# Ten plain single slices in front, a VectorE fill and a new hand-written order in a Strassen weight-gradient matmul

## The chip, the cores and the metric

The kernel runs on one core of one Trainium2 chip. The metric is device time in microseconds (us), the median of several executions. The core's engines are TensorE (PE, with its weight loads shown apart as PEld), VectorE (DVE), ScalarE (ACT), GpSimd (POOL) and SyncE (SP). Each has an instruction queue of its own that runs in order; semaphores tie the queues together.

## The reference

```python
batch, m, k, n = 16, 512, 1024, 768
input:       (16, 512, 1024) float32, randn
grad_output: (16, 512, 768)  float32, randn

def reference(input, grad_output):
    return np.einsum('bmk,bmn->kn', input, grad_output).astype(np.float32)
```

One product of a 1024 x 8192 matrix (the transposed input X) with an 8192 x 768 matrix (grad_output G). The contraction runs over 8192 rows, so every row is read once and everything is summed into one 1024 x 768 result.

## The kernel before

**Slices, pairs, loads.** The 8192 rows are 64 slices of 128 rows. A load is a pair of slices, 32 loads in all. The string `LOADS` (line 12) says what is done with each: `s` is plain, `P` goes through one level of Strassen's scheme in Winograd's form. Before, loads 0 to 3 and the last one are plain, the 27 between are Strassen pairs. All loads but the first slice are DMAs from the GpSimd queue that round float32 to bf16 on the way. Loads below `MERGED` (2 before) are fetched slice by slice (lines 175 and 177: 192 KB of gradient, 256 KB of input in bf16), the others in one DMA each for G and X with two adjacent rows per partition (lines 170 and 171). The very first slice and the second one's X come in float32 over the ACT and SP queues and are rounded by VectorE and ScalarE (`round_by`, line 217).

**Products.** X is cut in two halves of 512 columns, G in two halves of 384 columns. A plain slice gives products A, B, C, D: the four quadrants of the result. A Strassen pair gives seven products, named 1, A, B, C, 5, 6, 7, of which 5, 6, 7 and the late operands of B and C need sums of blocks that VectorE makes in bf16 (`sum_x` and `sum_g`, lines 195 to 213, three stages each: L199, L201, L203 and L209, L211, L213). Each product has four parts q = 0 to 3 of 128 result rows. So a plain pair is 2 x 4 x 4 = 32 matmuls of 128x128 by 128x384 and a Strassen pair is 7 x 4 = 28. Parts 1 and 2 of A lie across two PSUM banks, and each of their matmuls is issued in two pieces, 256 and 128 columns wide.

**Sums in PSUM and SBUF.** A product part is accumulated in one of the PSUM banks 3 to 7 for some slices and is then closed: by VectorE (`v`, adds the bank to the SBUF sum `acc` or `macc`, L367) or by ScalarE (`c`, copies it, L363). A copy is allowed when the bank was first filled with the older sum by ScalarE (`f`, L295). A bank can also be laid aside by ScalarE (`z`, L379) and added later by VectorE (`y`, L388, two SBUF operands). Part A stays in banks 0 to 2 through the whole run. At the end the products are combined: final closes on VectorE (L355, L356, L360), and four whole-sum additions on GpSimd (`w`, L395, two SBUF operands). Finished parts are stored by DMA from the SP queue (L342), the very last part in two pieces, 256 columns over the ACT queue and 128 over SP.

**Order.** There is no scheduler: the string `PLAN` (lines 15 to 80) is a list of tokens in the order in which instructions are emitted, and each engine runs its own in that order. `C0@7.1` means: one matmul of product C, part 0, opened in bank 7; `x2.30` the third X sum of load 30; `g0.5` the first G sum of load 5; `r0` the rounding number 0; `vC3`, `cB1`, `fC1@7`, `zcC2.20`, `yC2.20`, `wD1` the operations above. The last tokens are `... fB3@3+4 vD3 B0.2 D0.2 vB0 B3.4 vD0 B3.2 cB3`. A matmul that waits holds up all later ones. `SPARE_LOADS` adds an extra weight load before every second matmul from number 200 to 454.

**Buffers.** Ten loads and eight sets of sums are held. GpSimd has eight DMAs outstanding: it issues one when the one eight places before has landed.

Of the kernel before, what the change touches and what calls it, by code (L numbers as in the profile page):

```python
# [9 lines left out]
P = 128  # L10

LOADS = "ssssPPPPPPPPPPPPPPPPPPPPPPPPPPPs"
# [3 lines left out]
    "A0.1 A2.1 C0@7.1 A3.1 C2@6.1 cC0 r0 C3@3.1 C1@4.1 cC2 A1.1 vC3 B1@5.1 cC1 B2@7.1 D3@6.1 r1 D0@3.1 r4 r2 "  # L16
    "D1@4.1 cB1 D1.1 A0.1 B2.1 cD1 D0.1 B0@5.1 cD3 A3.1 vD0 A2.1 r3 A1.1 B3@6.1 vB0 cB2 B3.1 D3@4.1 B0@3.1 "
    "D2@7.1 vD3 D2.2 B0.1 vB3 B1@5.1 cD2 B1.1 A3.1 C3@4.1 vB1 C3.1 C2@6.2 vC3 A2.1 B3@7.1 C1@5.3 B3.1 B0.1 "
    "vC1 A1.2 C2.1 vB3 B1@4.1 D1@5.1 zcC2.20 D1.1 vB1 B2@7.2 A0.1 vB0 A0.1 A2.1 vD1 D3@6.2 D0@4.1 vB2 D0.1 "
    "A3.1 C3@5.1 vD0 D2@3.1 C0@7.2 vD3 C0.2 vD2 C0.1 C3.2 B3@6.2 vC3 B1@3.2 A3.1 vC0 D3@5.2 vB1 A1.2 B2@4.1 "  # L20
    "vD3 B2.1 D2@3.1 A0.1 yC2.20 A0.1 A3.1 D0@7.1 vB2 D0.1 A2.2 vD2 B0@5.2 D1@4.1 vD0 D1.3 vB0 C0@7.2 A3.1 "
    "vD1 A3.1 A1.1 vC0 B3.1 D2@5.3 fC1@7 B3.1 D0@4.1 vD2 D0.1 A0.2 vD0 fD3@5 C1.3 vB3 C1.1 A2.2 g0.4 cC1 "
    "C3@4.1 B2@6.1 fC2@3 B2.1 g1.4 D3.2 fB0@7 vB2 C3.1 C2.1 cD3 C2.1 g2.4 C2.1 x0.4 C2.2 A2.1 12@5.1 cC2 C3.1 "
    "x1.4 A1.2 c12 x2.4 11@6.1 C0@3.1 fC1@5 vC3 B0.3 c11 vC0 A3.1 C1.1 A0.1 B3@6.1 cC1 61@3.1 B1@4.1 vB3 cB0 "
    "B1.2 c61 73@5.1 g0.5 71@6.1 10@7.1 vB1 13@3.1 x0.5 13.1 A1.1 12@4.1 c13 10.1 A3.1 v12 71.1 c10 73.1 "
    "50@3.1 x1.5 c71 50.1 11@4.1 g1.5 51@7.1 c50 51.1 v11 60@6.1 c73 60.1 61@3.1 g0.6 c51 A2.1 53@5.1 v61 "
    "53.1 fC0@4 A0.1 63@7.1 c53 g2.5 63.1 52@3.1 g1.6 52.1 70@5.1 g2.6 70.1 c52 C0.1 x0.6 C0.1 A1.1 A3.1 cC0 "
    "72@3.1 x2.5 72.2 x1.6 70.1 73@4.1 A0.1 c70 x2.6 63.1 60.1 v73 A2.1 c63 B0@5.2 g0.7 c72 B2@4.2 c60 B2.1 "
    "vB0 62@7.1 fC1@3 62.1 g1.7 62.1 B3@6.1 vB2 B3.1 c62 C1.2 g2.7 C2@4.1 fC0@7 vB3 C2.2 f13@5 C1.1 x0.7 A2.1 "
    "A0.1 cC1 C0.1 11@6.1 vC2 11.1 f51@3 A1.1 13.1 v11 13.1 51.2 x1.7 c13 A3.1 53@6.1 cC0 x2.7 53.1 52@4.1 "  # L30
    "c51 52.1 v53 71@5.2 f50@7 C3@3.1 g0.8 C3.1 f12@6 C3.1 50.1 g1.8 50.1 12.1 g2.8 12.2 x0.8 A2.1 C3.1 c12 "
    "A1.1 A3.1 vC3 52.1 71.1 50.1 x1.8 zc52.20 73@6.2 v71 fB1@3 A0.1 61@4.2 x2.8 c50 61.1 72@5.1 v73 72.1 "
    "fB2@7 B1.2 v72 f10@6 B1.2 B2.1 v61 B2.1 cB1 63@5.1 g0.9 63.1 f51@4 10.3 fC2@3 x0.9 10.1 A1.1 cB2 A3.1 "
    "A2.1 g1.9 51.1 zc63.5 x1.9 51.1 62@7.1 c10 g2.9 62.2 x2.9 c51 A0.1 C2.1 v62 fB3@5 C2.1 60@6.2 y63.5 60.1 "
    "fB0@7 B3.2 v60 cC2 B3.1 11@4.2 y52.20 cB3 B0.2 f13@3 g0.10 B0.1 53@6.2 cB0 13.1 x0.10 13.2 f70@7 A3.1 "
    "11.1 g1.10 c13 A1.1 53.1 x1.10 70.1 f52@5 70.1 v11 70.2 A0.1 g2.10 fB2@4 52.1 x2.10 52.1 C1@3.1 c70 v53 "
    "C1.2 c52 B2.1 C3@7.1 vC1 C3.1 f72@5 B2.1 C0@6.1 vC3 C0.1 cB2 C0.1 72.1 g0.11 f73@3 B1@7.2 A2.1 c72 x0.11 "
    "A2.1 A1.1 f71@4 73.2 vC0 73.1 f63@5 71.1 g1.11 71.1 c73 71.1 x1.11 A0.1 72@6.1 c71 g2.11 72.1 63.1 x2.11 "
    "63.1 fB0@4 63.1 v72 61@3.2 c63 61.1 g0.12 B0.1 fC2@6 B0.1 60@5.1 v61 60.1 cB0 A3.1 g1.12 C2.2 v60 12@3.2 "
    "cC2 12.1 x0.12 12.1 fC3@4 B1.1 A1.1 A2.1 f53@5 g2.12 A3.1 vB1 C3.1 f51@6 C3.1 53.1 v12 53.1 cC3 50@7.2 "  # L40
    "x1.12 50.1 fC1@4 50.1 g0.13 A0.1 c53 51.2 x2.12 51.1 C1.1 g1.13 B3@5.1 c51 B3.1 v50 B3.1 f13@3 C1.1 "
    "52@6.1 vB3 52.1 cC1 13.2 x0.13 13.1 f62@4 11@5.2 c13 11.1 x1.13 A0.1 62.1 v52 62.1 f70@3 62.2 g2.13 "
    "61@7.2 c62 x2.13 70.2 v61 fC0@6 70.1 B2@4.2 v11 c70 B2.1 C0.2 vB2 f71@3 C0.1 A3.1 f73@7 10@5.1 g0.14 "
    "10.3 B1@4.1 x0.14 A2.2 zcB1.4 71.2 10.1 x1.14 f51@4 71.1 73.1 g1.14 73.1 c71 x2.14 73.1 51.1 g2.14 51.1 "
    "c73 A1.2 v10 c51 A0.1 B3@7.1 g0.15 cC0 B3.1 A3.1 63@3.1 vB3 fB1@6 63.2 B0@5.1 g1.15 f70@4 B0.1 v63 B0.1 "
    "B1.2 g2.15 72@7.2 cB1 vB0 72.1 70.1 C2@3.1 x0.15 f52@5 C2.3 53@6.2 vC2 53.1 70.1 52.1 v53 52.2 72.1 "
    "x1.15 f11@6 C1@3.2 v72 C1.1 c52 A2.1 A0.1 vC1 c70 13@7.2 60@5.1 yB1.4 f10@3 60.2 g0.16 60.1 11.2 x0.16 "
    "11.1 10.2 c11 13.1 v60 A1.2 f62@4 A3.1 x1.16 A3.1 f71@6 A2.1 v13 50@5.3 g1.16 50.1 f12@7 g0.17 62.2 "
    "zc50.18 62.1 12.1 g1.17 12.1 c62 12.1 g2.16 12.1 x2.16 71.1 fB1@4 71.1 g2.17 C3@5.1 c12 C3.1 x2.15 C3.2 "
    "x0.17 C3.1 10.1 A2.1 C0@7.1 c10 vC3 C0.2 c71 C0.1 x1.17 A3.1 A0.1 fB2@6 x2.17 A0.1 B0@3.1 g0.18 B0.2 "  # L50
    "B2.1 vC0 B2.3 vB0 B1.3 g1.18 C2@7.2 cB1 g2.18 73@5.2 cB2 vC2 73.1 C1@3.1 f61@4 C1.1 x0.18 C1.1 A1.1 "
    "zc73.3 51@6.2 vC1 51.2 C2@5.1 x1.18 fB3@3 61.2 vC2 61.3 x2.18 f53@5 63@7.2 g0.19 63.1 c61 63.1 53.2 v63 "
    "f52@4 53.1 B3.2 g1.19 f12@7 B3.1 v51 B3.1 A0.1 c53 52.1 12.1 cB3 12.1 13@5.1 x0.19 f71@6 13.2 12.1 "
    "72@3.1 x1.19 72.2 v13 72.1 71.2 v12 71.1 70@5.2 g0.20 70.1 f60@7 70.1 52.1 v72 52.2 60.1 g1.20 60.1 c52 "
    "x2.19 60.2 c71 A1.1 v70 A1.1 11@3.1 f10@6 g2.19 11.2 x0.20 11.1 fB3@5 10.3 v11 A3.2 c10 A3.1 x1.20 A2.1 "
    "fB1@3 73@4.1 x2.20 73.2 g0.21 B3.1 60.1 62@6.1 v73 62.1 c60 62.2 g2.20 B1.1 C0@4.1 g1.21 C0.1 cB1 y50.18 "
    "C0.1 C2@7.1 cB3 C2.1 g2.21 B1@3.2 v62 fB2@5 A2.3 x0.21 B2.3 vC0 C2.1 71@6.2 zcC2.1 vB1 A0.1 51@4.1 cB2 "
    "51.1 g0.22 51.1 A0.1 f72@5 50@7.1 v71 50.3 g1.22 50.1 C1@3.2 v50 C1.1 72.2 x1.21 C3@7.2 g2.22 c72 C3.1 "
    "v51 C3.2 C1.1 x0.22 A1.3 zcC1.10 12@6.1 f63@5 12.1 x1.22 12.1 53@4.1 f13@3 53.1 v12 53.2 63.1 x2.21 63.2 "
    "x2.22 63.1 B0@6.1 g0.23 B0.1 c63 B0.2 v53 B0.1 A0.1 vC3 A0.1 f70@4 13.3 f52@5 x0.23 13.1 70.2 c13 70.1 "  # L60
    "g1.23 A3.1 fC0@7 x1.23 A3.1 52.1 vB0 52.3 g2.23 61@3.2 g0.24 61.3 70.1 C0.1 v61 C0.1 c70 C0.1 62@6.1 "
    "y73.3 c52 62.2 cC0 x2.23 B3@4.3 g1.24 f71@5 B3.1 v62 A3.2 A0.1 x0.24 A0.1 A2.3 vB3 71.3 x1.24 73@4.2 "
    "yC1.10 c71 73.2 fB2@7 50@6.1 g2.24 50.1 v73 11@5.3 x2.24 B2.1 f60@4 B2.1 v11 B2.1 f62@3 B2.1 60.1 g0.25 "
    "60.1 cB2 60.2 x0.25 A1.3 72@7.1 x1.25 72.2 g1.25 72.1 A3.1 yC2.1 62.1 zc72.15 62.1 60.1 x2.25 A2.1 "
    "B1@5.1 c60 g2.25 B1.2 c62 B1.2 B0@4.1 f10@3 B0.1 vB1 B0.1 53@7.2 g0.26 53.1 10.2 g1.26 10.2 x0.26 10.2 "
    "51@5.2 c10 x1.26 51.2 y72.15 51.1 f52@3 50.1 A3.1 vB0 zc51.21 50.2 A0.1 x2.26 A0.1 fB2@4 63@5.1 g0.27 "
    "63.3 52.1 g1.27 53.1 v50 B2.2 zc53.18 52.1 v63 52.1 cB2 12@6.2 g2.26 12.2 x0.27 12.1 B3@7.2 g2.27 B3.1 "
    "11@4.1 v12 11.3 y53.18 C0@5.3 vB3 C0.1 C2@6.2 g0.28 fC3@7 C2.3 vC0 C2.1 C3.1 g1.28 C3.2 x1.27 C3.2 vC2 "
    "52.1 61@5.1 cC3 61.1 y51.21 61.1 c52 61.1 A2.1 v11 A2.2 13@6.1 x0.28 13.4 x1.28 72@7.2 zc13.12 72.1 "
    "x2.28 61.1 f73@3 70@4.1 v72 70.2 f71@6 70.1 v61 70.1 73.2 g2.28 73.1 x2.27 73.1 C3@5.1 g0.29 71.4 g1.29 "  # L70
    "A2.1 C1@7.1 c71 g2.29 C1.2 c73 x0.29 C1.4 A3.1 g0.30 A3.1 zcC1.4 A3.1 C3.1 f11@3 v70 A1.4 x1.29 f62@4 "
    "12@7.1 g1.30 12.1 A0.1 y13.12 A0.2 11.1 vC3 11.1 10@6.2 x0.30 10.2 11.1 13@5.1 v10 13.1 c11 12.1 62.1 "
    "x1.30 f61@6 62.2 v12 62.1 f72@3 62.1 61.1 v13 f71@7 61.1 A2.1 v62 72.1 f60@5 72.1 71.1 v61 71.1 f51@4 "
    "60.2 g2.30 60.1 f52@6 60.1 v72 60.1 51.2 v60 f70@3 51.1 wC2 51.1 52.1 v71 52.2 A3.1 f63@7 v51 A3.2 70.1 "
    "fC0@5 70.1 63.2 yC1.4 63.1 wD1 63.1 C0.1 v70 C0.1 fC1@4 C0.2 v63 C0.1 A0.2 vC0 fD1@7 A0.1 C1.2 v52 fC2@5 "
    "C1.1 A2.2 f73@3 A1.3 vC1 fB1@6 wD2 D1.2 x2.30 73.2 cD1 x2.29 B1.2 vA3 B1.1 fB2@7 B1.2 v73 fD2@4 B1.2 "
    "C2.1 vA2 C2.1 f53@3 C2.2 vA1 C2.1 53.2 cC2 53.1 vB1 53.1 B2.1 fC3@5 B2.1 v53 B2.1 fD3@2 B2.3 f50@6 C3.1 "
    "vA0 C3.2 wB3 50.1 vB2 50.3 vC3 D2.1 fB0@7 D2.1 D3.1 v50 D3.1 cD2 B0.2 fD0@5 B0.3 fB3@3+4 vD3 B0.2 D0.2 "
    "vB0 B3.4 vD0 B3.2 cB3 "
# [8 lines left out]
MERGED = 2  # L88
# [364 lines left out]
```

## Time and profile before

| what | value |
|---|---|
| median of 3 runs | 162.03 us (161.86 to 162.07) |
| the profiled execution, its own time | 161.87 us |
| its span, first to last instruction | 160.1 us |
| granted TensorE clock | 1.000 |
| PE busy | 154.8 us (97%), 1002 matmuls, 996 of them products |
| DVE busy | 145.1 us (91%), 335 instructions |
| ACT busy | 99.3 us (62%), 227 instructions |
| POOL busy | 39.1 us (24%) |
| DMA engines, mean busy tenths | 9 from 4 to 140 us, then little until the stores |
| DMA packets | 33.41 MB moved, 58.72 MB read from HBM |

The span begins with the first loads and a row of warm-up matmuls on constants. The first product starts at 5.04 us, the last ends at 156.73 us, and the last store has landed before 160.1 us. The profiled execution lies at the lower end of the three timed runs, 0.16 us under their median, and has 1.8 us around its span. Reading hints: a matmul's duration in the trace contains its way through the array, so the next one starts well before the one before has ended, and an engine's idle time counts only from that modelled end. A row "x4" in the timeline merges four instructions.

### The profile page before, as it was taken

Reading aid. Unit: us, or ns where it says so; the run is one execution under the profiler, and the core shown is the slowest. Engines: PE = TensorE matmul, PEld = TensorE weight load, DVE = VectorE, ACT = ScalarE, POOL = GpSimd, SP = SyncE. Lnnn points to the kernel's source line nnn. Section 1 sums busy time; section 2 is a strip of 40 time slices with the busy share of each in tenths; the row PEclk is TensorE's granted clock in tenths of the full one; section 3 lists DMA queues with packets and bytes.
Section 4 is the critical chain, followed back from the end, with each engine's and each line's share of the span. In section 5 each row is a group of like instructions: output and inputs, shape, how many; then the busy total and the mean of one; then the engine's idle time right before and its main releaser. Section 6 shows DMA issues by size and latency. Waiting matters only on the chain.

```text
span 160.1 us, 2989 instructions
## 1 busy us (share of the span) xinstructions
PE 154.8 (97%) x1002; PEld 98.9 (62%) x1129; DVE 145.1 (91%) x335; ACT 99.3 (62%) x227; POOL 39.1 (24%) x73
## 2 busy tenths in 40 slices
PE   8999999999999999999999999999999999999891
PEld 3466666567677777776656566666666566666461
DVE  0579899999999999999999999999989999999991
ACT  3741028779699998985785756365465244586760
POOL 7442212222221222222122222212222100024120
PEclk9999999999999999999999999999999999999999
DMA  5999999999999999999999999999999999930696
GB/s 176 296 211 212 214 215 215 212 213 216 209 214 214 212 211 214 214 213 214 213 214 213 213 212 212 214 214 209 214 214 212 214 213 214 213 60 18 184 365 218
DMA packets 12446, 33.41 MB, mean 209 GB/s; under 512 B 1424, under 2 KB 4240, under 8 KB 12432
## 3 DMA queue, kind: packets, MB, share of 16 engines
q0 software_dynamic: 9360, 28.64, 90.4%
q1 hardware_dynamic: 2640, 3.41, 6.6%
q10 hardware_dynamic: 432, 1.18, 2.0%
q8 instruction: 8, 0.13, 0.3%
q14 instruction: 6, 0.05, 0.1%
HBM read 58.72 MB, written 3.15 MB: 386 GB/s over the span
## 4 chain that ended last, share of the span: by engine, by line
PE 78%; DMA 16%; POOL 1%; DVE 1%; issue 1%; DVEq 0%; POOLq 0%
PE bank L324 78%; DMA xp<-in_input_dram 16%; POOL gp L175 1%; DVE xp L203 1%; POOL xp L177 0%; DVE acc L365 0%; DVEq L365 0%; POOLq L437 0%
## 5 line engine op out<-in xcount | busy, mean ns | idle before, releaser
L324 PE MATMUL bank<-gp,xp 128*128 128x384 bf16 (+2 forms) x672 | 108.9, 307 | 1.1 <-DVE xp L203 0.5
L324 PEld LDWEIGHTS <-xp 128*128 128x128 bf16 x672 | 61.7, 97 | 32.4 <-DMA xp<-in_input_dram 2.0
L324 PE MATMUL bank<-ge,xe 128*128 128x384 bf16 x324 | 64.0, 326 | 0.0
L324 PEld LDWEIGHTS <-xe 128*128 128x128 bf16 x324 | 31.2, 97 | 15.3 <-DVE xe L201 0.2
L363 ACT COPY macc<-bank 128x384 f32<-128x384 f32 x63 | 28.8, 482 | 17.5 <-PE bank L324 17.3
L367 DVE TENSOR_TENSOR acc<-bank,acc 128x384 f32<-128x384 f32 x62 | 32.4, 552 | 2.8 <-PE bank L324 2.6
L295 ACT COPY bank<-macc 128x384 f32<-128x384 f32 x60 | 28.2, 485 | 6.2 <-DVE macc L367 2.8
L367 DVE TENSOR_TENSOR macc<-bank,macc 128x384 f32<-128x384 f32 x55 | 29.9, 552 | 1.1 <-PE bank L324 0.6
L295 ACT COPY bank<-acc 128x384 f32<-128x384 f32 (+2 forms) x43 | 20.1, 478 | 14.7 <-DVE acc L367 12.1
L171 POOL DMA_DIRECT2D xp<-in_input_dram x30 | 15.9, 532 | 51.9 <-DMA xp<-in_input_dram 22.8
L170 POOL DMA_DIRECT2D gp<-in_grad_output_dram x30 | 16.0, 532 | 38.3 <-PE bank L324 18.8
L363 ACT COPY acc<-bank 128x384 f32<-128x384 f32 (+1 forms) x42 | 19.4, 479 | 8.2 <-PE bank L324 7.8
L199 DVE TENSOR_TENSOR xe<-xp 128x1024 bf16<-128x1024 bf16 x27 | 18.5, 685 | 0.1
L209 DVE TENSOR_TENSOR ge<-gp 128x768 bf16<-128x768 bf16 x27 | 14.8, 550 | 0.3 <-DMA gp<-in_grad_output_dram 0.3
L203 DVE TENSOR_TENSOR xp<-xp,xe 128x512 bf16<-128x512 bf16 x27 | 11.7, 440 | 0.2
L201 DVE TENSOR_TENSOR xe<-xe,xp 128x512 bf16<-128x512 bf16 x27 | 11.3, 419 | 0.3
L379 ACT COPY aside<-bank 128x384 f32<-128x384 f32 x13 | 6.2, 479 | 8.0 <-PE bank L324 7.8
L323 PEld LDWEIGHTS <-xp 128*128 128x128 bf16 x81 | 7.9, 98 | 4.8 <-DMA xp<-in_input_dram 0.4
L395 POOL TENSOR_TENSOR acc<-acc,macc 128x384 f32<-128x384 f32 x4 | 4.2, 1061 | 22.8 <-DVE macc L360 16.5
L211 DVE TENSOR_TENSOR ge<-gp,ge 128x384 bf16<-128x384 bf16 x27 | 9.5, 352 | 0.2
L213 DVE TENSOR_TENSOR gp<-ge,gp 128x384 bf16<-128x384 bf16 x27 | 9.5, 351 | 0.1
L360 DVE TENSOR_TENSOR acc<-bank,macc 128x384 f32<-128x384 f32 (+2 forms) x14 | 6.3, 489 | 0.1
(23 smaller groups left out, 37.6 us busy)
## 6 DMA issues: line engine op xcount, KB each, us to landing
xp<-in_input_dram POOLq DMA_DIRECT2D x30, 512.0 KB, 16.9
gp<-in_grad_output_dram POOLq DMA_DIRECT2D x30, 384.0 KB, 16.7
out_dram<-acc SPq DMA_DIRECT2D x12, 192.0 KB, 2.1
xf<-in_input_dram ACTq DMA_DIRECT2D x2, 512.0 KB, 4.9
gp<-in_grad_output_dram POOLq DMA_DIRECT2D x3, 192.0 KB, 6.5
out_dram<-acc SPq DMA_DIRECT2D x6, 96.0 KB, 2.2
xp<-in_input_dram POOLq DMA_DIRECT2D x2, 256.0 KB, 7.8
gf<-in_grad_output_dram SPq DMA_DIRECT2D x2, 192.0 KB, 4.4
```

What stands on the lines that cost most here:

```text
L170: nc.gpsimd.dma_start(out=gp, in_=G[rows, :].rearrange("(p m) n -> p m n", m=2))
L171: nc.gpsimd.dma_start(out=xp, in_=X[rows, :].rearrange("(p m) k -> p m k", m=2))
L199: nc.vector.tensor_sub(out=xe[:, 0:2, :], in0=x[:, 1::-1, :], in1=x[:, 3::-2, :])
L201: nc.vector.tensor_sub(out=xe[:, 2, :], in0=xe[:, 0, :], in1=x[:, 0, :])
L203: nc.vector.tensor_add(out=x[:, 1, :], in0=x[:, 2, :], in1=xe[:, 2, :])
L209: nc.vector.tensor_add(out=ge[:, 0:2, :], in0=g[:, 0:2, :], in1=g[:, 1::2, :])
L211: nc.vector.tensor_add(out=ge[:, 2, :], in0=g[:, 3, :], in1=ge[:, 0, :])
L213: nc.vector.tensor_add(out=g[:, 1, :], in0=ge[:, 2, :], in1=g[:, 2, :])
L295: nc.scalar.copy(out=tile_[:, t0 : t0 + c1 - c0], in_=sum_of(p, q)[:, c0:c1])
L324: nc.tensor.matmul(tile_[:, t0 : t0 + c1 - c0], stat, mov[:, c0:c1], start=start, stop=True, skip_group_check=True,)
L363: nc.scalar.copy(out=d, in_=b)
L367: nc.vector.tensor_add(out=d, in0=b, in1=d)
```

## The change

`LOADS` has five plain loads in front instead of four, and one Strassen pair fewer. `MERGED` goes from 2 to 5: loads 0 to 4, the plain ones in front, are now all fetched slice by slice. `fill` uses VectorE for a piece 128 columns wide; the only such piece is the second half of the last part, B3. The first seven roundings become tokens of the plan (`r10` to `r16`). `SPARE_LOADS` ends at 449. The plan is a new one altogether, 1166 tokens for 1230; all its matmuls, closes, fills and sums stand in new places. In the new plan the first GpSimd addition (`wC3`) is emitted after the last block sums (`x2.30`, `g2.30`); in the old one `x2.30` and `x2.29` follow `wD2`.

```diff
-LOADS = "ssssPPPPPPPPPPPPPPPPPPPPPPPPPPPs"
+LOADS = "sssssPPPPPPPPPPPPPPPPPPPPPPPPPPs"
 PLAN = (
-    "A0.1 A2.1 C0@7.1 A3.1 C2@6.1 cC0 r0 C3@3.1 C1@4.1 cC2 A1.1 vC3 B1@5.1 cC1 B2@7.1 D3@6.1 r1 D0@3.1 r4 r2 "
...
-    "C1.1 A2.2 f73@3 A1.3 vC1 fB1@6 wD2 D1.2 x2.30 73.2 cD1 x2.29 B1.2 vA3 B1.1 fB2@7 B1.2 v73 fD2@4 B1.2 "
-    "C2.1 vA2 C2.1 f53@3 C2.2 vA1 C2.1 53.2 cC2 53.1 vB1 53.1 B2.1 fC3@5 B2.1 v53 B2.1 fD3@2 B2.3 f50@6 C3.1 "
-    "vA0 C3.2 wB3 50.1 vB2 50.3 vC3 D2.1 fB0@7 D2.1 D3.1 v50 D3.1 cD2 B0.2 fD0@5 B0.3 fB3@3+4 vD3 B0.2 D0.2 "
-    "vB0 B3.4 vD0 B3.2 cB3 "
+    "r11 r10 r16 r14 r15 A1.1 r13 r12 A0.1 C2@7.1 C0@3.1 A2.1 A3.1 cC0 r0 vC2 D1@6.1 D3@5.1 r4 B2@4.1 r2 "
...
+    "x1.30 13@3.1 c10 A0.1 61.1 v13 61.2 71.1 x2.30 f62@3 60.2 v61 60.1 f72@4 60.1 62.1 v71 f63@7 62.1 72.2 "
...
+    "vA2 70.1 f50@3 wC3 70.2 vA1 70.1 53.2 vA0 53.1 wC1 fC3@4 53.2 v70 C0.1 f52@0 C0.2 v53 C0.1 fC1@7 50.3 "
+    "fD0@1 C3.2 vC0 C3.1 fB1@6 wD3 C1.2 v50 fD1@2 C1.1 D0.2 f51@5 52.1 wB3 52.1 cC1 52.1 yC2.3 D1.2 v52 51.1 "
+    "fD3@7 51.2 cC3 51.2 fD2@3 D3.1 vD0 D3.1 B1.1 fC2@4 B1.1 v51 B1.1 cD3 B1.1 D2.2 C2.1 fB2@7 C2.1 vD2 C2.1 "
+    "fB0@1 C2.1 B2.1 vB1 B2.1 fB3@3+0 B2.2 vD1 B2.1 B0.1 vC2 B0.3 vB2 B0.4 B3.2 vB0 B3.3 cB3 "
 ).split()
-MERGED = 2
-SPARE_LOADS = range(200, 455)
+MERGED = 5
+SPARE_LOADS = range(200, 450)
...
-    round_by("DVE", g0, gf, 0, 192)
-    round_by("ACT", g0, gf, 192, NH)
-    round_by("DVE", x0, xf[0], 0, P)
-    round_by("ACT", x0, xf[0], 2 * P, 4 * P)
-    round_by("DVE", x0, xf[0], P, 2 * P)
-    round_by("DVE", x0, xf[0], 4 * P, 6 * P)
-    round_by("ACT", x0, xf[0], 6 * P, 8 * P)
-    ROUNDINGS = [
-        ("DVE", g0, gf, NH, N),
...
+    ROUNDINGS = {
+        0: ("DVE", g0, gf, NH, N),
...
+        10: ("DVE", g0, gf, 0, 192),
+        11: ("ACT", g0, gf, 192, NH),
+        12: ("DVE", x0, xf[0], 0, P),
+        13: ("ACT", x0, xf[0], 2 * P, 4 * P),
+        14: ("DVE", x0, xf[0], P, 2 * P),
+        15: ("DVE", x0, xf[0], 4 * P, 6 * P),
+        16: ("ACT", x0, xf[0], 6 * P, 8 * P),
+    }
...
-            nc.scalar.copy(out=tile_[:, t0 : t0 + c1 - c0], in_=sum_of(p, q)[:, c0:c1])
+            copy = nc.vector.tensor_copy if c1 - c0 == 128 else nc.scalar.copy
+            copy(out=tile_[:, t0 : t0 + c1 - c0], in_=sum_of(p, q)[:, c0:c1])
```

Counted from the two plans, per engine:

| | before | after |
|---|---|---|
| product matmuls (pieces) | 916 (996) | 920 (1001) |
| block sums on DVE | 162 | 156 |
| additions of a bank or an aside sum on DVE, not final (L367, L388) | 130 | 123 |
| fills, ACT closes, lay-asides (tokens f, c, z) | 220 | 200 |
| DMAs issued by GpSimd | 65 | 71 |
| GpSimd additions | 4 | 4 |

## The prediction

> **What bounds the kernel now.** I read the page first (PE 97% busy, granted clock full throughout), then PE's waits, then PE, GpSimd and the end of the span in the timeline. PE's waits (us in total, times, longest):
>
> ```profile
> PE bank L324 <- DVE xp L203: 0.5, 1, 0.5
> PE bank L324 <- DMA xp<-in_input_dram: 0.4, 2, 0.3
> PE bank L324 <- DVE gp L217: 0.2, 1, 0.2
> ```
>
> Where they lie, and how fast PE runs without them (start, length, what, in brackets idle time before it):
>
> ```profile
> 5.04 1.49 PE L324 MATMUL bank<-gp,xp 128*128 128x384 bf16 x10
> 6.78 9.28 PE L324 MATMUL bank<-gp,xp 128*128 128x384 bf16 x62 [0.25 <-DVE gp L217]
> 16.23 12.22 PE L324 MATMUL bank<-gp,xp 128*128 128x384 bf16 x84 [0.17 <-DMA xp<-in_input_dram]
> ...
> 30.05 0.99 PE L324 MATMUL bank<-gp,xp 128*128 128x384 bf16 x6 [0.26 <-DMA xp<-in_input_dram]
> ...
> 139.43 1.30 PE L324 MATMUL bank<-ge,xe 128*128 128x384 bf16 x7
> ```
>
> Seven matmuls take 1.30 us and one lasts 0.326 (page), so starts are (1.30 - 0.326) / 6 = 0.162 us apart; a row of six (1.14 us) gives 0.163. I use 0.1625. An idle time of PE therefore costs itself plus 0.326 - 0.1625 = 0.16: the four waits cost 0.41 (at 6.78, rounding of G's right half), 0.34 and 0.42 (at 16.23 and 30.05, a load not landed) and 0.62 (at 149.22, VectorE's last block sums), 1.79 together. From 5.04 to the last matmul's end at 156.73, less 0.16 for its way out, are 151.53 us; 916 products x 0.1625, with 0.2 for the 80 that are cut in two, are 149.05. So 2.48 us are lost, and 0.69 beside the four lies in delays too short to show as idle. PE's work is the bound; only the lost 2.5 us, the tail and the number of products can move the end.
>
> GpSimd's queue tells when loads land: it waits for the landing eight DMAs back and issues 0.28 us later (the chain of waits has X of slice 3 landing at 3.50 + 8.41 = 11.91, the issue is at 12.20).
>
> ```profile
> 9.96 0.53 POOL L171 DMA_DIRECT2D xp<-in_input_dram  x1 [0.73 <-DMA xp<-in_input_dram]
> 10.91 0.53 POOL L170 DMA_DIRECT2D gp<-in_grad_output_dram  x1 [0.42 <-DMA gp<-in_grad_output_dram]
> 12.20 0.53 POOL L171 DMA_DIRECT2D xp<-in_input_dram  x1 [0.76 <-DMA xp<-in_input_dram]
> ...
> 16.47 0.53 POOL L171 DMA_DIRECT2D xp<-in_input_dram  x1 [1.93 <-DMA xp<-in_input_dram]
> 18.33 0.53 POOL L170 DMA_DIRECT2D gp<-in_grad_output_dram  x1 [1.32 <-DMA gp<-in_grad_output_dram]
> 20.83 0.53 POOL L171 DMA_DIRECT2D xp<-in_input_dram  x1 [1.97 <-DMA xp<-in_input_dram]
> 23.76 0.53 POOL L170 DMA_DIRECT2D gp<-in_grad_output_dram  x1 [2.40 <-DMA gp<-in_grad_output_dram]
> 25.97 0.53 POOL L171 DMA_DIRECT2D xp<-in_input_dram  x1 [1.68 <-DMA xp<-in_input_dram]
> ```
>
> A single slice takes 0.95 (G) + 1.29 or 1.26 (X) = 2.22 us, a merged pair 1.86 + 2.50 = 4.36 (16.47 to 20.83). The step to 23.76 is 2.93 where 1.86 is usual, the next 2.21 where 2.45 to 2.50 is: all later landings are 0.8 late. The queue's DMA list for 20 to 25 us has one instruction packet, 16 KB, 1.2% of 16 engines x 5 us = 0.96 us of one engine: a fetch of instructions that holds one of the 16 up.
>
> The end (the tail is from the last matmul to the last store):
>
> ```profile
> 144.59 0.55 DVE L388 TENSOR_TENSOR acc<-acc,aside 128x384 f32<-128x384 f32 x1
> 144.75 1.25 POOL L395 TENSOR_TENSOR acc<-acc,macc 128x384 f32<-128x384 f32 x1 [1.13 <-DVE macc L356]
> 147.54 1.00 POOL L395 TENSOR_TENSOR acc<-acc,macc 128x384 f32<-128x384 f32 x1 [1.54 <-DVE macc L356]
> 147.84 1.31 DVE L203 TENSOR_TENSOR xp<-xp,xe 128x512 bf16<-128x512 bf16 x2
> 156.85 0.29 DVE L365 COPY acc<-bank 128x128 f32<-128x128 f32 x1 [0.33 <-PE bank L324]
> ```
>
> The two L203 sums at 147.84 took 0.979 and 0.412 us, where 27 average 0.440 with the slow one: the first began during a GpSimd addition and ended 0.28 after it. Three rows up the reverse: an aside addition was first, and the GpSimd addition took 1.25 instead of 1.00. Both VectorE instructions have two SBUF operands; additions with a PSUM operand beside GpSimd kept their 0.55.
>
> **The change part by part.** *One Strassen pair made plain:* 4 products more, 4 x 0.1625 = **+0.65**, on the path. VectorE loses six block sums and 7 other additions; ScalarE loses 20 fills and closes. Both lie beside PE and only add slack. Three spare weight loads fewer (0.1 us each) lie beside matmuls: 0.
>
> *Start:* before, eight products (A0 A2 C0 A3 C2 C3 C1 A1) stand ahead of the first that needs G's right half (B1); now six (A1 A0 C2 C0 A2 A3) stand ahead of D1. That half is rounded by the same cast after the same landing, so PE goes on at 6.78 again, two products behind: 2 x 0.1625 = **+0.33**. (A0 also waits 0.17 for its cast, third in VectorE's new order; that lies inside.)
>
> *Slices:* six DMAs become twelve, 6 x 0.53 = 3.2 us more on GpSimd, which idled 0.4 to 2.0 before each issue; nothing else is in its queue then. Eight outstanding half-size DMAs are about 8.9 us of transfers, and the slices now took 6.5 to 7.8 to land, so the engines stay fed. Landings: slice 4 at 11.91 + 2.2 = 14.1, then 16.3, 18.5, 20.7, and with the 0.8 of the fetch 23.7 and 25.9; pairs 5, 6, 7 and 10 at 30.3, 34.6, 38.9 and 51.9 (4.32 each, the usual 1.86 + 2.46). PE reaches the first product of slices 4 to 9 after 53, 65, 79, 93, 111 and 124 products, at 6.78 + (n - 6) x 0.1625 = 14.4, 16.4, 18.6, 20.9, 23.8 and 26.0: always 0.1 to 0.3 after the landing. So both load waits go, **-0.76**. Pairs 5, 6, 7 and 10 are reached after 150, 176, 202 and 282 products, at 30.2, 34.4, 38.6 and 51.6, up to 0.3 before their landing: PE runs into the landings again, bounds 0 and 0.5 (slices at 2.24), taken **+0.2**.
>
> *Block sums off the GpSimd additions:* the 0.979 becomes about 0.41, **-0.57**. It is sure: the sum that the first GpSimd addition needs (closed by v73) stands behind the last block sum in VectorE's queue.
>
> *Short delays:* 0.69 before, some of it beside landings of pairs 6 to 8, which I have priced; VectorE and ScalarE have 5 to 9% less to hand over, but in a wholly new order. Bounds 0.2 and 0.9; I keep 0.31, **-0.38**.
>
> *Tail:* in the new plan VectorE's queue near the end has v53 (two additions), vC0, v50 (two), then the aside addition yC2.3; GpSimd starts wD3 when v53 is done and wB3 after it. VectorE's additions start 0.47 apart, so from v53's second start yC2.3 comes at 4 x 0.47 = 1.87, and wB3 runs from 0.55 + 0.08 + 1.0 = 1.63 to 2.63: yC2.3 falls into it and is held 0.7, as the L203 was. Behind it on VectorE stand eleven additions and the 128-wide fill (0.2 of queue; ScalarE did it before), 5.3 us; PE has 54 products, 8.8 us, from 53's end. VectorE's last addition, vB0, then ends 0.5 after PE instead of 0.1 before, its store follows, and SP issues stores 0.5 apart: the last store, now issued 0.44 after PE's end, slips by up to 0.6. If the addition isn't held, by nothing. PE itself isn't held: B3's first product is 11 products behind its fill. Between 0 and 0.6 I take **+0.3**.
>
> The Trainium skill ("SBUF — State Buffer", section "SBUF: two separate sides") says that GpSimd and a VectorE instruction with two SBUF inputs share a port pair under an exclusive lock, held for the whole instruction by whichever comes first. Both rows above agree. By this rule yC2.3 is held to wB3's end, and the sum would have 0.6 here instead of 0.3; without it, 0.
>
> Sum: 0.65 + 0.33 - 0.76 + 0.2 - 0.57 - 0.38 + 0.3 = -0.23. On the profiled execution 161.87 - 0.23 = 161.64; that run lies 0.16 under the median, so on the median of 162.03 it is **161.8**.
>
> **Rivals.** *The aside addition costs nothing* (VectorE is 0.3 early, so that GpSimd waits instead, or has slack from fewer additions): -0.53, 161.5. For: 5 us less work on VectorE. Against: its queue in the last 10 us is as dense as before.
>
> *Landings set the pace and slip (the slower side):* pairs 5 to 10 are met with no margin, so a second fetch on the late engine costs its whole 0.8: 162.6. It decides as soon as pair 10 lands later than 52.5 rather than 51.9. For: the page counts eight such packets, and 2.2 per slice rests on two slices. Against: GpSimd's issues after 26 us keep 4.3 per pair.
>
> *New handovers:* a different order makes one or two new waits of the present size (0.4 to 0.6) on a close or fill: 162.3. For: every bank changes hands in a new place. Against: VectorE's slack.
>
> That the block sum still collides is ruled out by the order.
>
> **How the numbers follow.** 0.2%, about what a measurement can tell here, is 0.32 us: faster is under 161.71, slower over 162.35. Forecast (161.6 to 162.1) 0.34: 0.10 faster, 0.24 same. Aside addition free (161.2 to 161.7) 0.31: 0.30 faster, 0.01 same. Landings (162.2 to 162.8) 0.21: 0.05 same, 0.16 slower. Handovers (162.1 to 162.6) 0.14: 0.05 same, 0.09 slower. Together 0.40, 0.35, 0.25. The range is 161.2 to 162.7, from the free tail to most of the landings case.
>
> **What would show it.** PE: first right-half product at 6.78 with 0.4 idle before it; no idle at 16 or 30; no L203 over 0.5; the first GpSimd addition after the last block sum. VectorE: yC2.3 near 1.0 us beside the last GpSimd addition, and the last stores 0.5 apart. It is wrong if PE shows idle over 0.3 between 7 and 150 us, if slices land over 2.3 apart, or if yC2.3 is not stretched.

## The result, and the profile after

| | before | after |
|---|---|---|
| median | 162.07 us (161.86 to 162.35, 13 runs) | 163.01 us (161.96 to 163.16, 13 runs) |
| ratio after / before | | 1.0049, interval 1.0038 to 1.0061 |
| profiled execution, its own time | 161.87 us | 162.31 us |
| its span | 160.1 us | 160.5 us |
| last matmul ends / last store lands / span ends | 156.72 / 159.19 / 160.1 | 156.70 / 159.62 / 160.5 |

The change makes the kernel slower by 0.5%, 0.94 us on the medians; 161.8 had been forecast, with a range up to 162.7. The thirteen runs of after lie in two groups, two at 161.96 and 162.31 and eleven at 162.80 to 163.16, and the profiled execution belongs to the two. Busy time from the page of after, and PE's waits of after (in total, times, longest):

```profile
PE 154.8 (96%) x1007; PEld 99.8 (62%) x1132; DVE 140.0 (87%) x323; ACT 91.5 (57%) x206; POOL 41.9 (26%) x79
```
```profile
PE bank L321 <- DVE gp L213: 0.7, 1, 0.7
PE bank L321 <- DVE xp L213: 0.4, 1, 0.4
```

Product matmuls are L321 now (L324 before), casts L213, GpSimd additions L392, additions of an aside sum L385. Both waits lie ahead of 7.3 us; no load and no block sum stands among PE's waits any more. PE in the timeline of after:

```profile
5.22 1.30 PE L321 MATMUL bank<-gp,xp 128*128 128x128 bf16 x8 [0.41 <-DVE xp L213]
7.21 24.41 PE L321 MATMUL bank<-gp,xp 128*128 128x384 bf16 x163 [0.69 <-DVE gp L213]
```

G's right half of slice 0 landed at 6.77 in this execution and at 6.35 in that of before, hence 7.21 instead of 6.78; from there to the last product the timeline shows no idle time of PE. To find where the usual 0.9 us lies, an execution of the larger group was needed: the first experiment.

### The profile page after: what moved, and what is told of

It reads as the page before. It is cut to its first block, busy times and chain, and to the rows that moved or that the text cites. A ratio compares the mean times of both kernels' runs of the same rounds, so it can differ in the third digit from the quotient of the medians.

```text
span 160.5 us, 2979 instructions
## 1 busy us (share of the span) xinstructions
PE 154.8 (96%) x1007; PEld 99.8 (62%) x1132; DVE 140.0 (87%) x323; ACT 91.5 (57%) x206; POOL 41.9 (26%) x79
## 4 chain that ended last, share of the span: by engine, by line
PE 91%; DMA 3%; DVE 2%; issue 1%; SPq 0%; DVEq 0%
PE bank L321 91%; DMA gf<-in_grad_output_dram 3%; DVE acc L357 1%; DVE macc L353 0%; SPq L141 0%; DVE gp L213 0%; DVE bank L292 0%; DVE macc L352 0%; DVEq L445 0%; DVEq L357 0%; DVEq L362 0%
## 5 line engine op out<-in xcount | busy, mean ns | idle before, releaser
L321 PE MATMUL bank<-gp,xp 128*128 128x384 bf16 (+2 forms) x689 | 110.8, 307 | 1.1 <-DVE gp L213 0.7
L321 PEld LDWEIGHTS <-xp 128*128 128x128 bf16 x689 | 64.5, 98 | 32.8 <-DVE xp L213 1.5
L321 PE MATMUL bank<-ge,xe 128*128 128x384 bf16 x312 | 62.1, 326 | 0.0
L321 PEld LDWEIGHTS <-xe 128*128 128x128 bf16 x312 | 29.9, 97 | 14.2 <-DVE xe L197 0.3
L364 DVE TENSOR_TENSOR acc<-bank,acc 128x384 f32<-128x384 f32 x56 | 29.9, 552 | 9.1 <-PE bank L321 8.7
L360 ACT COPY macc<-bank 128x384 f32<-128x384 f32 x59 | 27.1, 481 | 14.3 <-PE bank L321 13.4
L364 DVE TENSOR_TENSOR macc<-bank,macc 128x384 f32<-128x384 f32 x52 | 28.2, 553 | 0.9 <-PE bank L321 0.4
L360 ACT COPY acc<-bank 128x384 f32<-128x384 f32 (+1 forms) x35 | 16.2, 475 | 17.9 <-PE bank L321 17.6
L167 POOL DMA_DIRECT2D xp<-in_input_dram x27 | 14.3, 530 | 44.6 <-DMA xp<-in_input_dram 19.8
L166 POOL DMA_DIRECT2D gp<-in_grad_output_dram x27 | 14.3, 530 | 36.1 <-PE bank L321 23.6
L292 ACT COPY bank<-acc 128x384 f32<-128x384 f32 (+1 forms) x35 | 16.4, 482 | 9.4 <-DVE acc L364 6.3
L320 PEld LDWEIGHTS <-xp 128*128 128x128 bf16 x76 | 7.4, 98 | 4.6 <-DMA xp<-in_input_dram 0.3
L392 POOL TENSOR_TENSOR acc<-acc,macc 128x384 f32<-128x384 f32 x4 | 3.9, 1000 | 20.7 <-DVE macc L357 19.8
L320 PEld LDWEIGHTS <-xe 128*128 128x128 bf16 x49 | 4.8, 98 | 2.7
```

Of the source, the lines that this page charges most:

```text
L166: nc.gpsimd.dma_start(out=gp, in_=G[rows, :].rearrange("(p m) n -> p m n", m=2))
L167: nc.gpsimd.dma_start(out=xp, in_=X[rows, :].rearrange("(p m) k -> p m k", m=2))
L292: copy(out=tile_[:, t0 : t0 + c1 - c0], in_=sum_of(p, q)[:, c0:c1])
L320: nc.tensor.ldweights(stat)
L321: nc.tensor.matmul(tile_[:, t0 : t0 + c1 - c0], stat, mov[:, c0:c1], start=start, stop=True, skip_group_check=True,)
L360: nc.scalar.copy(out=d, in_=b)
```

## The experiments

Each was timed against the kernel before on the same chip; the ratio is the figure to compare, since the medians of before were 161.91 (the first three), 161.98 (the next four) and 161.94 (the last two).

### Again: the changed kernel once more, unedited

> The changed kernel itself, once more, to see where its usual 163.0 us (the profiled execution took 162.31) comes from. Theory L (a load lands late on PE, which follows the landings closely): an execution near 163.0 shows PE idle or short delays of 0.5 us or more between 10 and 60 us, and a load landing 0.5 us or more later than in the profile at hand. Theory S (the start): an execution near 163.0 has lost 0.5 us or more beyond the 0.85 us wait at 6.2 us before 8 us, and nothing after. Theory C (TensorE's clock): matmul starts over 0.1625 us apart somewhere, granted clock below 1. Theory T (the tail): the last matmul ends near 156.7 as in the profile at hand and the tail is 0.7 us longer than its 3.8 us.

162.81 us median (162.79 to 162.98, 4 runs), ratio 1.0057 (1.004 to 1.0074); profiled execution 162.79, span 161.0. PE in its timeline:

```profile
5.21 1.25 PE L321 MATMUL bank<-gp,xp 128*128 128x128 bf16 x8 [0.61 <-DVE xp L213]
6.78 14.39 PE L321 MATMUL bank<-gp,xp 128*128 128x384 bf16 x98 [0.32 <-DVE gp L213]
22.06 10.26 PE L321 MATMUL bank<-gp,xp 128*128 128x384 bf16 x65 [0.89 <-DMA xp<-in_input_dram]
```

G's right half came at 6.34 here and PE went on at 6.78, as forecast. The new row is the last: PE idles 0.89 for an X load, and loses 1.05 us with the 0.16 that the modelled end of a matmul hides. PE had done 93 products and needed slice 7. Its landing is read from GpSimd's queue; after in the first fence, this execution in the second:

```profile
19.79 0.53 POOL L166 DMA_DIRECT2D gp<-in_grad_output_dram  x1 [0.42 <-DMA gp<-in_grad_output_dram]
21.05 0.53 POOL L167 DMA_DIRECT2D xp<-in_input_dram  x1 [0.73 <-DMA xp<-in_input_dram]
22.91 0.53 POOL L166 DMA_DIRECT2D gp<-in_grad_output_dram  x1 [1.34 <-DMA gp<-in_grad_output_dram]
```
```profile
19.78 0.53 POOL L166 DMA_DIRECT2D gp<-in_grad_output_dram  x1 [0.42 <-DMA gp<-in_grad_output_dram]
22.29 0.53 POOL L167 DMA_DIRECT2D xp<-in_input_dram  x1 [1.98 <-DMA xp<-in_input_dram]
22.82 0.54 POOL L166 DMA_DIRECT2D gp<-in_grad_output_dram  x1
```

An issue stands 0.28 after the landing eight DMAs back, so slice 7's X landed at 20.76 in after and at 22.01 here, 1.25 later. In after the next transfer is the late one, slice 8's G at 22.63, 0.9 behind its usual 0.95 after the X; it is 22.5 here, and from there on the two run alike. What differs is the moment of the 16 KB packet of the instruction queue (q8). DMA queues from 20.1 to 20.4 us in after, and from 19.8 to 20.1 us here (packets, MB, share of 16 engines):

```profile
q0 software_dynamic: 41, 0.05, 98.7%
q8 instruction: 1, 0.02, 19.5%
```
```profile
q0 software_dynamic: 37, 0.06, 104.1%
q8 instruction: 1, 0.02, 19.5%
```

One packet takes 19.5% of 16 x 0.3 us = 0.94 us of one engine. It starts at 20.27 in after and at 19.96 here, and slice 7's X, whose first engine is done at 20.2, is the transfer that it just misses or hits. In both executions, and in two variants below, it starts when PE has begun 213 matmuls and weight loads that the trace records (229 in before, in another order, at 21.36): the fetch follows PE's progress. So a late right half (6.77) costs 0.4 at the start, moves the fetch 0.3 later and saves 1.05; the usual one (6.34) starts PE sooner and brings the fetch onto slice 7's X. Seven profiled executions of this order and its variants sort by it:

| execution | right half lands | fetch starts | slice 7's X lands | time |
|---|---|---|---|---|
| after | 6.77 | 20.27 | 20.76 | 162.31 |
| aside | 6.68 | 20.26 | 20.68 | 161.86 |
| warm_aside | 6.65 | 20.19 | 20.71 | 161.75 |
| again | 6.34 | 19.96 | 22.01 | 162.79 |
| warm | 6.16 | 20.01 | 22.03 | 162.80 |
| late7 | 6.36 | 20.00 | 22.05 | 162.10 |
| late7_aside | 6.00 | 20.01 | 22.03 | 161.89 |

(late7 and late7_aside use slice 7 later, below.) This is a match of times: no run moved the landing of the right half by itself, and what sets it is open.

### Aside: the aside addition moved clear of the GpSimd addition

```diff
-52.1 wB3 52.1 cC1 52.1 yC2.3 D1.2 v52 51.1
+52.1 wB3 52.1 cC1 52.1 D1.2 v52 yC2.3 51.1
```

> The aside addition yC2.3 stands behind v52 in VectorE's queue instead of ahead of it, so that it comes after the last GpSimd addition; all else as changed. If the hold of that addition (1.15 us instead of 0.55) is what lengthens the tail: tail 3.4 us instead of 3.8, 0.4 us less than the changed kernel, about 162.6. If the tail is set by the queue of stores alone: no difference (163.0).

162.65 us median (161.86 to 162.96, 10 runs), ratio 1.0037 (1.0021 to 1.0053). Its profiled execution has the late right half, and so stands beside after's 162.31: 161.86. The last two GpSimd additions (one row) and the aside addition on VectorE, first in after, then here:

```profile
149.18 1.96 POOL L392 TENSOR_TENSOR acc<-acc,macc 128x384 f32<-128x384 f32 x2 [0.95 <-DVE macc L353]
...
150.41 1.15 DVE L385 TENSOR_TENSOR acc<-acc,aside 128x384 f32<-128x384 f32 x1
```
```profile
148.97 1.95 POOL L392 TENSOR_TENSOR acc<-acc,macc 128x384 f32<-128x384 f32 x2 [0.95 <-DVE macc L353]
...
151.44 0.55 DVE L385 TENSOR_TENSOR acc<-acc,aside 128x384 f32<-128x384 f32 x1
```

The instruction took 1.15 us beside GpSimd and ended 0.42 after GpSimd's 151.14; alone it takes 0.55. With it 0.6 shorter the last store is issued at 157.02 instead of 157.44, and the time falls by 0.45. Of that, 0.40 lies in the tail, from PE's last matmul to the end of the span: 3.84 us in after, 3.44 here, 3.39 in before. That is one pair of executions; the pair late7 and late7_aside repeats it below, and by the ratios the medians fall by only 0.2 to 0.3. The edit has a price too: in all three profiled executions with it (aside, warm_aside, late7_aside) PE's starts show a delay of 0.15 at 153.2 that no other has; its cause was not traced.

### Merged: loads 2 to 4 in one DMA each for G and X again

```diff
-MERGED = 5
+MERGED = 2
```

> Loads 2 to 4 in one DMA each for G and X again (MERGED = 2), all else as changed. If the single slices are what keeps PE from waiting at the plain loads: PE, which reaches slice 4 near 14.9, waits for the pair's landing at 16.2, and again at slices 6 and 8: 1.0 to 1.7 us slower than the changed kernel, about 164.3. If single slices cost more on the DMA side than they bring: the same or up to 0.4 us faster.

163.73 us (163.56 to 163.99, 4 runs), ratio 1.0112 (1.0096 to 1.0128). In its timeline:

```profile
5.21 9.48 PE L321 MATMUL bank<-gp,xp 128*128 128x128 bf16 x60
16.37 16.87 PE L321 MATMUL bank<-gp,xp 128*128 128x384 bf16 x111 [1.68 <-DMA xp<-in_input_dram]
```

PE is ready for load 2 at 14.4, and its X lands at 16.3. Without the single slices PE loses 1.84 us at this one place, not again at slices 6 and 8 as expected: it is so far behind the loads after it that the fetch (at 21.82 here) shows no wait. By the ratios the run is 0.9 us slower than again, less than the 1.0 to 1.7 expected; that fits the 1.05 at slice 7 being gone as well.

### Warm: two warm-up matmuls fewer

```diff
-WARMUP = [("b", 512), ("f", 512), ("f", 512), ("b", 512)]
+WARMUP = [("f", 512), ("f", 512)]
```

> The changed kernel without the two bf16 warm-up matmuls: four PE instructions fewer ahead of the first product. Theory (the instruction fetch comes at a fixed count of started PE instructions, about 215, and the landing that it meets decides): the fetch comes two products, 0.33 us, later, at about 20.3 instead of 19.96; slice 7's X lands at 20.8 instead of 22.0, PE shows no idle time near 22, and the median is 162.0 to 162.3. Rival (the fetch is tied to the clock time, or the late slice has another cause): the idle time of 0.9 near 22 stays, 162.7 to 162.9.

163.1 us (161.99 to 163.47, 6 runs), ratio 1.0061 (1.0037 to 1.0085): the expectation missed. The right half landed early in the profiled execution (6.16), the fetch came at 20.01 and slice 7's X at 22.03. A shift of two products is no larger than the spread of that landing, so this run neither speaks for the theory nor against it.

### Warm_aside: both edits

> The same, with the aside addition yC2.3 moved behind v52, clear of the last GpSimd addition. If the two costs are independent: warm's time less the 0.3 to 0.4 of the tail, 161.6 to 161.9, no faster than the kernel before by more than 0.2. If the wait at 20.8 is not removed: 162.5 to 162.7.

162.69 us (161.75 to 163.19, 12 runs), ratio 1.0042 (1.0026 to 1.0058): as aside alone. Two of the twelve runs are under 162, the profiled one among them, with its fetch at 20.19. The median falls in the second case expected, 162.5 to 162.7 with the wait at slice 7 still there.

### Early: 24 weight loads more before the fetch

```diff
-                if begun_matmuls[0] in SPARE_LOADS and begun_matmuls[0] % 2:
+                if begun_matmuls[0] % 2 and (begun_matmuls[0] in SPARE_LOADS or 20 <= begun_matmuls[0] < 68):
```

> The changed kernel with 24 extra weight loads before products 20 to 67, which only raise the count of PE instructions. Theory (fixed count): the fetch comes about 12 products, 2 us, earlier, near 18.0; slice 6's X lands about 1 us late (19.6 instead of 18.55) and PE waits for it near 18.7 to 19.6 instead of for slice 7 at 20.8; slice 7 itself is then late by about as much as slice 6. Total 162.7 to 163.0, the wait moved. Rival (fixed time, or bytes of the load queue): the fetch stays near 20.0 and the wait stays at 20.8.

162.46 us (162.24 to 162.63, 8 runs), ratio 1.0027 (1.0017 to 1.0037): instructions added to the busiest engine, and about 0.4 us faster than the changed kernel by the ratios. The fetch came at the same count of 213 PE instructions, 12 matmuls sooner, at 18.75. Of the 0.75 after the expected 18.0, about 0.4 is this execution's right half, landed at 6.72; the rest is that those 12 matmuls take 1.47 us in again, where 2 had been reckoned. The fetch (18.6 to 18.9 us), GpSimd's queue and PE in the timeline:

```profile
q8 instruction: 1, 0.02, 19.8%
```
```profile
19.01 0.53 POOL L167 DMA_DIRECT2D xp<-in_input_dram  x1 [0.73 <-DMA xp<-in_input_dram]
21.07 0.53 POOL L166 DMA_DIRECT2D gp<-in_grad_output_dram  x1 [1.53 <-DMA gp<-in_grad_output_dram]
21.91 0.53 POOL L167 DMA_DIRECT2D xp<-in_input_dram  x1 [0.31 <-DMA xp<-in_input_dram]
```
```profile
7.16 14.33 PE L321 MATMUL bank<-gp,xp 128*128 128x384 bf16 x98 [0.42 <-DVE gp L213]
21.68 10.26 PE L321 MATMUL bank<-gp,xp 128*128 128x384 bf16 x65 [0.19 <-DMA xp<-in_input_dram]
```

Slice 6's X was on time (18.73); the transfer hit is the next one, slice 7's G (20.79, 1.3 late), and the X behind it is 0.9 late (21.63) instead of 1.25. PE waits 0.19, which costs 0.35. The fetch follows the count of instructions, not the time. The expectation was wrong about the place of the wait, because the fetch came too late for slice 6, and about the total, 162.7 to 163.0.

### Bsums: the kernel before without its first GpSimd addition

```diff
-    "C1.1 A2.2 f73@3 A1.3 vC1 fB1@6 wD2 D1.2 x2.30 73.2 cD1 x2.29
+    "C1.1 A2.2 f73@3 A1.3 vC1 fB1@6 D1.2 x2.30 73.2 cD1 x2.29
...
-D3.1 v50 D3.1 cD2 B0.2
+D3.1 v50 D3.1 vD2 B0.2
```

> The kernel before without its first GpSimd addition wD2 (D2 is closed by a VectorE addition instead of a copy), so that no GpSimd addition runs beside the last block sums. Theory (the slow block sum costs PE 0.6 and nothing else hides behind it): the L203 sum takes 0.41 instead of 0.98, the idle time near 149 is gone, and the median is 0.4 to 0.6 lower, 161.3 to 161.6. Rival (a next wait, on the close of the bank or on VectorE's queue at the end, takes its place): 161.8 to 162.1.

161.9 us (161.74 to 162.02, 11 runs), ratio 0.9994 (0.9985 to 1.0002): the rival. In its timeline the two block sums are both short, and PE's row goes through where before it stopped at 149.22:

```profile
148.00 0.75 DVE L203 TENSOR_TENSOR xp<-xp,xe 128x512 bf16<-128x512 bf16 x2
...
148.27 2.17 PE L324 MATMUL bank<-gp,xp 128*128 128x384 bf16 x12
```

PE's last matmul starts 0.41 sooner than in before, and the last store is issued at 156.88 instead of 157.17, yet it lands at 159.18 instead of 159.19. The DMA engines' busy tenths and rates from 150 to 160 us, in 40 slices, before and then here:

```profile
DMA  5492889999999999999999999996999999600000
GB/s 135 117 221 62 209 203 338 363 369 375 350 381 363 381 344 369 369 381 356 356 375 369 369 363 381 357 369 240 363 381 369 326 359 320 170 0 0 0 0 0
```
```profile
DMA  9278398999999999999999999999999999800000
GB/s 227 62 190 191 86 209 240 381 363 344 381 369 381 332 393 357 393 332 387 350 387 350 369 381 332 393 369 375 338 381 363 381 330 328 250 8 0 0 0 0
```

From 152 us on the stores keep the 16 engines at 9 tenths on average and about 365 GB/s, one 192 KB store each 0.53 us. PE's gain closed the gap in that row (the 6 with 240 GB/s) and nothing more. So in this kernel the train of stores sets the end once PE is done early enough.

### Late7: slice 7 used nine products later

```diff
-A3.2 vB2 A3.2 D2.1 vC2 D2.1 C0@7.5 B1@5.2 vC0 B1.2 A0.1 yB1.0 D1@7.6 B1.1 A0.1 A1.3 D0.3
+A3.2 vB2 A3.1 D2.1 vC2 A1.1 D0.1 C0@7.4 B1@5.2 C0.1 vC0 B1.1 A3.1 D2.1 B1.1 A0.1 yB1.0 D1@7.6 B1.1 A0.1 A1.2 D0.2
```

> The changed kernel with the same products in a slightly other order: seven products of slices 4 to 6 are moved ahead of the first use of slice 7, so that it comes 9 products, 1.5 us, later (product 103 for 94). Theory (the usual 163.0 is PE waiting about 1.05 for slice 7's X, late by the instruction fetch): the fetch stays near 20.0, slice 7's X still lands near 22.0, PE shows no idle time there, and 162.79 less 1.05 plus 0 to 0.4 for pairs that PE now meets earlier gives 161.75 to 162.15, with a spread of runs as small as that of the kernel before. Rival (the lost time only moves to slice 8 or pairs 5 to 7, whose landings are 0.8 late as well): a new wait of 0.6 to 0.9 between 23 and 45, 162.5 to 162.8.

162.35 us (162.1 to 162.66, 11 runs), ratio 1.0027 (1.0018 to 1.0036); profiled execution 162.10. Its GpSimd queue and PE in the timeline:

```profile
22.33 0.53 POOL L167 DMA_DIRECT2D xp<-in_input_dram  x1 [2.12 <-DMA xp<-in_input_dram]
```
```profile
6.80 24.50 PE L321 MATMUL bank<-gp,xp 128*128 128x384 bf16 x163 [0.32 <-DVE gp L213]
```

Slice 7's X is as late as in again (22.05), the start is the same, and PE runs past it. The median lies between the two forecasts, above the theory's 162.15. Of the 1.05 us, 0.69 stays gained between the two profiled executions; 0.42 comes back between 25 and 45 us in delays too short for an idle row. At landings lies 0.14 of it (starts 34.40 and 34.62 around pair 6's X, landed 34.58; 43.22 and 43.46 around pair 8's, landed 43.42); the other delays were not traced. A second fetch of 16 KB starts at 39.57, so what makes pair 8 late was not separated either. The two groups of runs are gone as well: they now span 0.56 us instead of 1.2.

### Late7_aside: both costs taken away

> The same with the aside addition yC2.3 moved behind v52, clear of the last GpSimd addition. Theory (the two costs are all that made the changed kernel slower, and they add): 0.3 to 0.45 under late7, 161.3 to 161.75, faster than the kernel before by 0.2 to 0.6. Rival (the train of stores, 0.53 apart, sets the end once PE is done earlier): as late7, no faster than before.

162.03 us (161.89 to 162.41, 11 runs), ratio 1.0008 (0.9999 to 1.0016); profiled execution 161.89. The aside addition takes 0.55 again, and the edit is worth 0.32 on the medians, 0.21 on the profiled executions (0.36 of tail, less the 0.15 of PE): the costs add. The expected 161.3 to 161.75 was missed, because late7 itself came out higher. Together the two edits bring the new order level with the kernel before, not under it. Whether the stores set the end here too was not tested.

## Why the prediction was wrong

The sum of the prediction beside the usual execution (again, 162.79, against before's 161.87; PE's lost time is what the space between two starts exceeds the usual one by):

| term | forecast | measured |
|---|---|---|
| 4 products more | +0.65 | +0.65 |
| start, two products fewer before the right half | +0.33 | +0.34 |
| load waits at 16.23 and 30.05 gone | -0.76 | -0.72 |
| landings set the pace | +0.2 | +1.05 |
| block sum off the GpSimd addition | -0.57 | -0.62 |
| short delays | -0.38 | -0.21 |
| tail | +0.3 | +0.42 |
| sum | -0.23 | +0.91 of +0.92 |

**The step that failed** is the landings one: "Landings: slice 4 at 11.91 + 2.2 = 14.1, then 16.3, 18.5, 20.7, and with the 0.8 of the fetch 23.7 and 25.9 ... always 0.1 to 0.3 after the landing", and the +0.2 with bounds 0 and 0.5 that rests on it. The landings up to 18.5 and after 23.7 were right to 0.25 in every profiled execution with single slices. The fetch was put behind slice 7 because in before it shows between 20 and 25 us, in the DMA list of a 5 us window, and I carried it over at that time. It belongs to PE's progress: in before it starts at 21.36, in the new order at 19.96, and the transfer that it hits is slice 7's X, whose usual landing at 20.76 is 0.1 to 0.2 us before PE needs it. The 0.89 idle is the prediction's own sign of being wrong, PE idle over 0.3 between 7 and 150 us. The margins of 0.1 to 0.3, which I had worked out, were the reason to ask what moves the fetch by 1 us; a narrower window would have given 21.36 and the count of PE instructions at it, and the plan gives the product at which that count is reached. Shown: the fetch's moment against slice 7's landing in seven executions, its shift by added instructions (early), and the gain when PE doesn't need slice 7 then (late7).

**The rival "landings set the pace and slip"** had the sign and the mechanism, a fetch's lateness met without margin, but it asked for a second fetch and for pair 10 after 52.5. Pair 10's X landed at 51.8 in again; the first fetch was enough, one slice earlier than assumed, and cost 1.05 rather than 0.8 because here the transfer that is hit ends 1.25 late and only those behind it 0.8.

**Right:** PE goes on at 6.78 with 0.32 idle before it (0.4 forecast) where the right half lands as in before. The first product starts 0.17 later, at 5.21 instead of 5.04: its 128-wide cast, second in VectorE's queue, took 0.378 where the one in that place took 0.227 in before. This lies within the wait for the right half. No idle row stands at 16 or 30. The block sums are all short: the third X sum averages 0.42 in after, and none is over 0.43:

```profile
L199 DVE TENSOR_TENSOR xp<-xp,xe 128x512 bf16<-128x512 bf16 x26 | 10.8, 420 | 0.3
```

The single slices were worth about their price of 0.76: merged loses 1.84 without them, but not the 1.05 at slice 7, and is 0.9 slower than again.

**Smaller differences.** The spare weight loads go from 127 to 125, two fewer and not three, at the same price of nothing. Of the short delays 0.48 was left where 0.31 had been kept.

**The tail** was right in its mechanism and near in size: yC2.3 fell into the GpSimd addition and took 1.15 instead of 0.55. The Trainium skill ("SBUF — State Buffer", section "SBUF: two separate sides") states this as an exclusive lock that the instruction which comes first holds to its end. The trace agrees: the stretch is the 0.6 that the prediction gave by this rule. About 0.4 of it reached the end, between the 0.3 taken and the 0.6.

**Block sum and start** need a reservation that the prediction lacked. Bsums shows that in the kernel before the 0.57 can't be had alone: behind the train of stores 0.01 of it is left at the last landing. And the start's 0.33 may be worth little by itself: in late7, where PE is earlier, it loses 0.42 between 25 and 45 us, part of it at the landings of pairs 6 and 8. That last is argued; an earlier start was not tried.

## What to carry to other kernels

Where PE meets each load with 0.1 to 0.3 us to spare, look for what can make one transfer late, and find out what moves it: here an instruction fetch that comes at a fixed count of PE instructions, not at a fixed time, so each new order puts it on another load. Put the slack at the load that it hits (nine products later was worth 0.7 us in PE and halved the spread) rather than evenly. Before pricing a gain of PE near the end, look whether the stores behind it already run back to back.

## What the runs showed of the hardware

- One 16 KB fetch on the instruction queue takes 0.94 us of one of 16 DMA engines. The transfer that it hits lands 0.9 late in after, 1.25 in again and 1.3 in early, and the loads behind it 0.8 to 0.9 late.
- It comes at 213 recorded PE instructions in four executions of the changed order and its variants (209 to 215 in all of them), and moved from 19.96 to 18.75 us with 24 weight loads added, so a kernel got faster by more work.
- Where G's right half landed at 6.77 the changed kernel took 162.31, and where it landed at 6.34, 162.79: the execution with the load 0.4 later was 0.5 faster. The seven executions above agree with this order of events; no run tests it by itself.
- The 128-wide cast that the first product waits for took 0.378 us in again, 0.252 in after and 0.207 in early, with the same casts in the same order on VectorE (0.227 in before); the cause of the spread is open.
- Stores of 192 KB each follow one another at 0.53 us, about 365 GB/s; with PE's last start 0.41 sooner the last of them landed 0.01 sooner (before and bsums).
